# A hybrid decoder trunk on one core: the five steps of an S5 head reordered, its weight loads on another queue

## The chip, the cores and the metric

The kernel runs on one core of one Trainium2 chip. The metric is the device time of the whole kernel in microseconds (us), taken as the median of several runs; less is better. TensorE (PE; PEld is its weight load), VectorE (DVE), ScalarE (ACT) and GpSimd (POOL) each work through a list of instructions of their own; SyncE (SP) issues most of the DMA transfers.

## What is computed

One layer on a sequence of 1024 tokens of width 1024. The part that the change touches is the S5 branch, a linear recurrence with complex diagonal states; beside it stand large matrix products.

```
h = RMSNorm(x);  s5_x, s5_gate, lru_x, lru_gate, gate_s, gate_l = split(h @ W_in)
# S5: 32 groups of 16 channels, 64 complex states each
a_bar = exp(lam * dt);  b_bar = (a_bar - 1) / lam * b
state[t] = a_bar * state[t-1] + b_bar @ u[t]
y = Re(C state) + D * u
z_s = (glu(gelu(y) @ W_glu) * silu(s5_gate)) @ W_bs
z_l = (rg_lru(conv(lru_x)) * silu(lru_gate)) @ W_bl
mix = (sigmoid(gate_s) * z_s + sigmoid(gate_l) * z_l) @ W_out
x = x + RMSNorm(mix);  x = x + (p @ W_ple) * sigmoid(x @ W_ple_gate)
```

All inputs and the output are float32.

## The kernel before

**The products.** Each matrix product is built of 128x128 weight blocks. A float32 operand is split into a high part (a copy rounded to TensorE's fp32r format) and a low part (the rest), and a product is three matmuls: high by high, high by low, low by high (`three`, L327-331). The class `Weights` (from L145) loads raw weight blocks (`wraw`, L172, on SP's queue), makes the high half on ScalarE (L232) and the low half on DVE (L245) or, for some blocks, on ScalarE and a GpSimd DMA (L236, L237). Weights are made in quads of four blocks in a ring of six, four quads ahead of their use; a raw buffer comes free when the low half is made.

**The rows and the background.** `rows` computes one row of 128 output channels by 1024 tokens: eight weight blocks, two halves of 512 tokens, three matmuls each. After every second block it calls `tick()`, which advances each generator in the list `bg` by one step. All instructions of TensorE, DVE, ScalarE and GpSimd run in the order in which this code issues them, so a step of a generator lands between two pieces of a row. The order of SP's transfers is set by a planner, which places them by its own costs and due times; each waits on SP until what it needs is there. While 13 gate rows are computed (u3, two with SiLU, eight and two with a sigmoid, each followed by `light`'s sigmoid L1034 and a store L1038), the generator `s5_all` (L1008) carries the S5 branch.

**The S5 branch** in its order:
- `s5_params` (prep): small operations on the parameters. Its powers times zoh (`powers_zoh`, seven DVE operations, L681-687) go to `pzt` in page 3; GpSimd makes the input matrix `bb_1` of kernel taps with scratch `bt` (L693-695).
- `s5_ladders`: tables of cosines and sines in page 6, built by doubling (DVE, L720-729), in three pieces.
- `turn` (L699): TensorE transposes the powers (`pwT`), ScalarE copies them, and SP writes them to DRAM (`pt_d`, L706).
- `s5_load(hb)` (L892): the weights `wn` of head hb: two loads of powers from `pt_d`, replicated over 16 channels (L897), one load of B from the input `sbt` (L899), and the head's input `U` (L903). All on SP's queue; `wn` takes pages 2 and 3 in turn.
- `s5_table(hb)` (L875): cosines and sines of the head, DVE, in three steps (L883, L886-887).
- `s5_out_weights(hb)` (L909): output weights `ca`, three GpSimd products of 1.2 to 1.5 us, with scratch `t9` that shares a buffer (tag `kt`) with the tile `kt`.
- `s5_main(hb)` (L921), five steps, one a tick: (1) the product of `wn` with B (DVE, L928, L930), `dd` (GpSimd); (2) the end of the head before (`before()`: `py`, L999-1000, GELU L1002, stores of y), loads of the next head, `pkt` (L944), `pin` (L948), kernel taps `kt` copied by ScalarE (L950) and sent out in eight transfers to the Toeplitz tile `toep` (L953), a step of the next table; (3) `pq` (ScalarE, L962), rotation into `q` (DVE, L966-969), the next `ca`; (4) four scans (L976), a table step, rotation back (L980-981); (5) `q` shifted (L987-988), a table step.

There are eight heads of four groups each.

**Behind the heads** come products for six gate columns by Winograd's scheme (Strassen's with fewer additions): `lprod` on X (`xs`, copied to `lu` by ScalarE, L1145), then on Z and W. Its operands are differences T1 to T4 of quarters of h. The quarters are read back from DRAM (`h_load`, L1088); the differences are taken by `t_subs` on DVE (L1067), the high parts by `t_high` (ScalarE, L1063), the low parts by `t_low` (DVE, L1058). `t_early` does T1 and T2 from head six on, then T3 and T4; `t_build` makes the rest beside the first products. `lu` lies in page 15, which is opened over the memory that the S5 branch and the gate rows' output tiles used.

Of the kernel before, what the change touches and what calls it, by code (L numbers as in the profile page):

```python
# [17 lines left out]
P = 128  # L18
# [245 lines left out]
def tile_hybrid_trunk(  # L264
# [286 lines left out]
    def s5_params():  # L551
# [116 lines left out]
        def wide(t, sign):  # L668
            if sign:
                s_ = take(32)  # L670
                G.tensor_tensor(s_, t, sgn.to_broadcast([P, 32]), ALU.mult)
                t = s_
            return t.unsqueeze(2).to_broadcast([P, 32, 16])

# [3 lines left out]
        z_r, z_i = (t.unsqueeze(1).to_broadcast([P, 8, 32]) for t in (zr, zi))  # L678
        rv, iv = (t[:, 7::-1, :] for t in (pw_r, pw_i))
        def powers_zoh():  # L680
            V.tensor_tensor(pz[:, 0], rv, z_r, ALU.mult)  # L681
            V.tensor_tensor(pt_[:, 0], iv, z_i, ALU.mult)
            V.tensor_tensor(pz[:, 0], pz[:, 0], pt_[:, 0], ALU.subtract)
# [3 lines left out]
            V.tensor_tensor(pz[:, 1], pz[:, 1], sgn.unsqueeze(2).to_broadcast([P, 8, 32]), ALU.mult)  # L687

        turned.extend((powers_zoh, pzt))
        yield  # L690
        b1, b2, bt = (g32(braw[:, 512 * j:512 * j + 512]) for j in range(3))
        zrb, zis = wide(zr, False), wide(zi, True)
        G.tensor_tensor(bb_1, b1, zrb, ALU.mult)  # L693
        G.tensor_tensor(bt, b2, zis, ALU.mult)
# [4 lines left out]
    def turn():  # L699
        pzt = turned[1]  # L700
        ps = px.tile([P, HT], F32, tag="px", name="pwT")
        for n in range(4):
            T.transpose(ps[:, n * P:(n + 1) * P], pzt[:, n * P:(n + 1) * P], ident)
        pzs = pzt[:, 1024:1536]
        S.activation(pzs, ps, AF.Copy)
        nc.sync.dma_start(pt_d.rearrange("r (h q) (g n) -> (q g) (r h) n", h=2, n=P),  # L706
                          pzs.rearrange("p (m n) -> p m n", n=P))
# [5 lines left out]
    def s5_ladders():  # L713
        t = page(6, "etab", F32)
        e1 = t[:, :512].rearrange("p (r i n) -> p r i n", r=2, i=16)
        e2 = t[:, 512:768].rearrange("p (r i n) -> p r i n", r=2, i=16)
        tm = t[:, 768:1024].rearrange("p (r i n) -> p r i n", r=2, i=16)
        e_tab[1], e_tab[2] = e1, e2
        for e, m0, steps in ((e1, 1, 4), (e2, 5, 3)):
            V.memset(e[:, 0, :, 0:1], 1.0)  # L720
            V.memset(e[:, 1, :, 0:1], 0.0)
# [170 lines left out]
    def s5_load(hb):  # L892
        if hb > 7:
            return
        t = page(2 + hb % 2, f"wn{hb}", F32).rearrange("p (s r n) -> p s r n", s=2, r=2)
        for r in range(2):
            nc.sync.dma_start(t[:, 0, r],  # L897
                              pt_d[r, :, HT * hb:HT * hb + HT].unsqueeze(0).to_broadcast([16, 8, HT]))
# [5 lines left out]
        wload[hb] = t, U  # L904
# [16 lines left out]
    def s5_main(hb, table, before):  # L921
# [5 lines left out]
        wn, U = wload.pop(hb)  # L927
        V.tensor_tensor(wn[:, 0], wn[:, 0], wn[:, 1], ALU.mult)  # L928
        win = wn[:, 0, 0].rearrange("p (g n) -> p g n", g=4)
        V.tensor_tensor(wn[:, 0, 0], wn[:, 0, 0], wn[:, 0, 1], ALU.subtract)  # L930
        dd = wk.tile([16, 4, 16], F32, tag="dd", name=f"dd{hb}")
        G.tensor_tensor(
            dd, ident[:16, :16].unsqueeze(1).to_broadcast([16, 4, 16]),
            d_skip[:, 4 * hb:4 * hb + 4].unsqueeze(2).to_broadcast([16, 4, 16]), ALU.mult)
# [3 lines left out]
        s5_load(hb + 1)  # L938
        if hb == 7:
            h_load(2, "T2", "B22")  # L940
        kt = wk.tile([P, 576], F32, tag="kt", name=f"kt{hb}")[:16, :HT].rearrange("p (g m) -> p g m", g=4)
# [9 lines left out]
        V.tensor_tensor(kt[:, :, 0:16], kt[:, :, 0:16], dd, ALU.add)  # L951
        for j in range(8):
            nc.sync.dma_start(toep[j::8, :, 16 * j:P], kt[:, :, 0:P - 16 * j])  # L953
        if hb == 7:
            h_load(6, "T4", "B21")
        next(table, None)
        yield

        pq = wk.tile([P, 4, P], F32, tag="pq", name=f"pq{hb}").rearrange("p (r i) n -> p r i n", r=2)
# [10 lines left out]
        if hb < 7:  # L970
            s5_out_weights(hb + 1)
        yield

        for r in range(2):
# [14 lines left out]
        next(table, None)  # L989
        yield  # L990

        def finish():
            for _ in table:
                pass
# [56 lines left out]
    lop = {"T2": [3, 19], "T1": [9, 16], "T3": [17, 2], "T4": [7, 8]}  # L1051
# [13 lines left out]
    def t_subs(n, a, b):  # L1065
        for k in range(4):
            V.tensor_tensor(lf[n][:, k], lf[a][:, k], lf[b][:, k], ALU.subtract)  # L1067
            if k % 2:
                yield

    def t_early():
        yield from t_subs("T1", "T1", "T3")
        while "T2" not in lf:
            yield
        yield
        yield
        yield from t_subs("T2", "T2", "T1")
        t_high("T2")
        t_high("T1")
        lpage("T2", 1)  # L1080
        t_low("T2")
        yield
        while "T4" not in lf:
            yield
        yield from t_subs("T3", "T2", "T3")
        yield from t_subs("T4", "T4", "T2")
# [21 lines left out]
    def t_build():  # L1108
        lpage("T1", 1)
        t_low("T1")  # L1110
        yield
        t_high("T3")
        lpage("T3", 1)
        lpage("T4", 0)
        for k in range(4):
            S.activation(lop["T4"][0][:, k, :], lf["T4"][:, k], AF.Copy)
        yield
        t_low("T3")
        yield
        lpage("T4", 1)  # L1120
# [711 lines left out]
```

## Time and profile before

| | us |
|---|---|
| median of 3 runs | 941.76 (939.78 to 941.83) |
| the profiled execution, whole | 942.38 |
| its span, first to last instruction | 940.6 |
| TensorE busy | 915.2 |
| DVE busy | 664.9 |
| ScalarE busy | 493.1 |
| GpSimd busy | 150.3 |

The page of the profile gives busy times, groups of instructions by line, and the chain of work that ended last. The view of waits lists who waited for whom: engine, the waiting line, the releaser, then total us, times, and the longest. The view by stretches gives busy time per engine between two moments. A timeline row is start us, duration us, engine, line, operation, output and inputs, count, and in brackets the idle time before it and what ended it.

### The profile page before, as it was taken

The page shows a single profiled execution, that of the slowest core. Times are in us where ns is not written, and L with a number is a line of the kernel's source. Part 1 is how long each engine was busy: PE and PEld are TensorE (multiplying, and loading weights), DVE is VectorE, ACT ScalarE, POOL GpSimd, SP SyncE. Part 2 cuts the span into 40 slices and gives each one's busy share as a digit, 9 for nine tenths or more (in the row PEclk, how much of TensorE's full clock was granted, in tenths as well). Part 3 has the DMA queues.
Part 4 walks back from the last instruction along what each step waited for, and adds up shares of the span by engine and source line. Part 5 has one row for each costly group of instructions (what it writes and reads, how often), then busy time and mean ns, then how long its engine had stood idle before and what let it go on. Part 6 is the DMA issues. An engine that isn't in the chain of part 4 may idle for free.

```text
span 940.6 us, 11829 instructions
## 1 busy us (share of the span) xinstructions
PE 915.2 (97%) x4192; PEld 757.1 (80%) x4192; DVE 664.9 (71%) x1050; ACT 493.1 (52%) x763; POOL 150.3 (16%) x148
## 2 busy tenths in 40 slices
PE   9999799999989999999999999999999999999998
PEld 7887587877868888888888888888888887878887
DVE  6878787978674326777666676777863698786863
ACT  6643235434754236666666667544534255557541
POOL 1316122232100000000000000011331216522100
PEclk9999899999999999999999999999999999999999
DMA  9786656575655311111111115731469976399951
GB/s 356 299 254 209 185 158 175 142 206 171 166 154 172 101 51 49 35 46 51 51 50 51 51 45 179 253 127 34 146 213 271 257 187 206 113 241 236 273 200 64
DMA packets 76298, 146.53 MB, mean 156 GB/s; under 512 B 18896, under 2 KB 33360, under 8 KB 76240
## 3 DMA queue, kind: packets, MB, share of 16 engines
q1 hardware_dynamic: 69328, 132.68, 44.3%
q0 software_dynamic: 6768, 12.85, 7.7%
q8 instruction: 33, 0.54, 0.2%
q10 hardware_dynamic: 144, 0.26, 0.1%
q14 instruction: 25, 0.20, 0.1%
HBM read 101.06 MB, written 31.72 MB: 141 GB/s over the span
## 4 chain that ended last, share of the span: by engine, by line
PE 74%; DVE 8%; DMA 7%; issue 5%; ACT 4%; POOL 1%; SPq 0%; ACTq 0%; POOLq 0%; DVEq 0%
PE ps_rg L331 8%; PE ps_rx L331 8%; PE ps_pg L331 6%; PE ps_L L331 5%; PE ps_rx L329 4%; PE ps_rg L329 4%; PE ps_pg L329 3%; PE bZ L331 3%; PE ps_L L329 3%; PE ps_u L331 2%; DMA wn<-pt_d 2%; PE bX L331 2%; PE pg L331 2%; PE bW L331 2%; PE lZ L331 2%
## 5 line engine op out<-in xcount | busy, mean ns | idle before, releaser
L331 PE MATMUL ps_L<-hB,wq 128*128 128x512 f32 x448 | 139.3, 392 | 0.0
L232 ACT ACTIVATE wq<-wraw 128x512 fp32r<-128x512 f32 (+1 forms) x191 | 114.5, 613 | 30.0 <-DMA wraw<-w_blocks 10.3
L245 DVE TENSOR_TENSOR wq<-wraw,wq 128x512 fp32r<-128x512 f32 (+1 forms) x146 | 101.3, 709 | 14.7 <-ACT wq L232 14.7
L331 PEld LDWEIGHTS ps_L<-hB,wq 128*128 128x128 f32 x448 | 85.1, 190 | 17.9 <-DVE wq L245 0.3
L331 PE MATMUL ps_rx<-hB,wq 128*128 128x512 f32 x320 | 98.6, 389 | 0.0
L331 PE MATMUL ps_rg<-hB,wq 128*128 128x512 f32 x320 | 98.6, 389 | 0.0
L329 PE MATMUL ps_L<-hB,wq 128*128 128x512 f32 x224 | 89.0, 398 | 0.0
L331 PE MATMUL ps_pg<-x1hl,wq 128*128 128x512 f32 x240 | 74.8, 392 | 1.1 <-DMA wq<-wraw 1.1
L1212 DVE SCALAR_TENSOR_TENSOR c<-ps_rx,cp_t,c 128x1023 f32<-128x1023 f32 (+2 forms) x30 | 38.5, 1282 | 48.9 <-ACT c L1210 48.2
L331 PEld LDWEIGHTS ps_rx<-hB,wq 128*128 128x128 f32 x320 | 60.1, 188 | 12.5
L331 PEld LDWEIGHTS ps_rg<-hB,wq 128*128 128x128 f32 x320 | 60.1, 188 | 12.5
L237 POOL DMA_DIRECT2D wq<-wraw x45 | 39.6, 879 | 167.0 <-ACT wq L236 136.3
L204 POOL TENSOR_TENSOR wS<-wraw 128x512 f32<-128x512 f32 x8 | 12.2, 1519 | 333.9 <-DMA wraw<-w_blocks 322.3
L329 PE MATMUL ps_rx<-hB,wq 128*128 128x512 f32 x160 | 62.2, 389 | 0.0
L329 PE MATMUL ps_rg<-hB,wq 128*128 128x512 f32 x160 | 62.2, 389 | 0.0
L331 PEld LDWEIGHTS ps_pg<-x1hl,wq 128*128 128x128 f32 x240 | 44.9, 188 | 11.8 <-DMA wq<-wraw 2.1
L329 PEld LDWEIGHTS ps_L<-hB,wq 128*128 128x128 f32 x224 | 42.7, 190 | 8.5
L329 PE MATMUL ps_pg<-x1hl,wq 128*128 128x512 f32 x120 | 46.9, 391 | 0.0
L331 PE MATMUL ps_u<-hB,wq 128*128 128x512 f32 x128 | 39.8, 392 | 0.4 <-DVE hB L774 0.4
L331 PE MATMUL ps_F<-ys,wq 128*128 128x512 f32 x128 | 39.4, 389 | 0.0
L1220 ACT ACT_TABLE_LOAD x9 | 11.5, 1283 | 51.4 <-DVE yr L1249 51.4
L329 PEld LDWEIGHTS ps_rg<-hB,wq 128*128 128x128 f32 x160 | 30.0, 188 | 6.2
(394 smaller groups left out, 2114.5 us busy)
## 6 DMA issues: line engine op xcount, KB each, us to landing
wraw<-w_blocks SPq DMA_DIRECT2D x98, 512.0 KB
wq<-wraw POOLq DMA_DIRECT2D x45, 256.0 KB, 5.7
xt<-x_t SPq DMA_DIRECT2D x8, 512.0 KB
ple_d<-ple_sb SPq DMA_DIRECT2D x8, 512.0 KB
h_d<-xt SPq DMA_DIRECT2D x8, 512.0 KB
wn<-sbt SPq DMA_DIRECT2D x8, 512.0 KB
fT<-h_d SPq DMA_DIRECT2D x4, 1024.0 KB
wn<-pt_d SPq DMA_DIRECT2D x16, 256.0 KB
```

The costliest lines, as they stand in the source:

```text
L204: (self.nc.vector if light else G).tensor_tensor(s[name], s[a], s[b], op)
L232: nc.scalar.activation(hi, src, AF.Copy)
L237: nc.gpsimd.dma_start(lo.bitcast(F32), src, accum_op=ALU.add)
L245: self.nc.vector.tensor_tensor(lo, src, hi.bitcast(F32), ALU.subtract)
L329: T.matmul(ps, wh, xh, start=start, stop=False, skip_group_check=more)
L331: T.matmul(ps, a, b, start=False, stop=stop and a is (wh if xl_last else wl), skip_group_check=more)
L1212: V.scalar_tensor_tensor(c[:, d:], ps[:, :NT - d], w_[3 - d], c[:, d:], ALU.mult, ALU.add)
L1220: S.activation(sq, ps, AF.Sigmoid)
```

## The change

- The powers lose their seventh operation (the sign goes into two small GpSimd products ahead of them) and run inside `prep`; `bt` moves from the page of B to the second half of `pzt`, where the powers' scratch was.
- `turn` writes `pt_d` from ScalarE's queue. The loads of `wn` are split into `s5_raw` (B) and `s5_pow` (powers), both on ScalarE's queue; `U` stays on SP's.
- The ladders are dealt out in five pieces, not three.
- `t9` gets room of its own in page 6; `kt` is a plain tile.
- The five steps of a head: (1) loads of the next `wn`, a table step; (2) end of the head before, `pkt`, `pin`, `kt`, Toeplitz transfers, the next `U`, the next `ca`, a table step; (3) `pq`, `q`, the rest of the table; (4) scans, rotation back, the next `dd`; (5) `q` shifted, then the product of the next `wn`.
- One tick more ahead of the first head.
- T1 and T3 are loaded at heads one and two, T1's differences are taken one at a time at heads three to six, T2 and T4 are loaded in head six, `t_early` starts at head seven and does T2 alone; T3's and T4's differences and T1's high parts go to `t_build`.
- `lu` lies in page 9; T1's operands in pages 16 and 17, T3's in 15 and 2.

```diff
+        zrs, zis_ = take(32), take(32)
+        G.tensor_tensor(zrs, zr, sgn.to_broadcast([P, 32]), ALU.mult)
+        G.tensor_tensor(zis_, zi, sgn.to_broadcast([P, 32]), ALU.mult)
...
-            V.tensor_tensor(pz[:, 1], rv, z_i, ALU.mult)
-            V.tensor_tensor(pt_[:, 1], iv, z_r, ALU.mult)
+            V.tensor_tensor(pz[:, 1], rv, z_is, ALU.mult)
+            V.tensor_tensor(pt_[:, 1], iv, z_rs, ALU.mult)
             V.tensor_tensor(pz[:, 1], pz[:, 1], pt_[:, 1], ALU.add)
-            V.tensor_tensor(pz[:, 1], pz[:, 1], sgn.unsqueeze(2).to_broadcast([P, 8, 32]), ALU.mult)
...
+        bt = g32(pzt[:, 512:1024])
...
-        nc.sync.dma_start(pt_d.rearrange("r (h q) (g n) -> (q g) (r h) n", h=2, n=P),
+        nc.scalar.dma_start(pt_d.rearrange("r (h q) (g n) -> (q g) (r h) n", h=2, n=P),
...
-        e_tab[1], e_tab[2] = e1, e2
+        e_tab[1], e_tab[2], e_tab[9] = e1, e2, t[:, 1024:1600]
...
-                if m % 2 and m0 == 1:
+                if m and m0 == 1 or m == 1:
                     yield
...
+    def s5_raw(hb):
         t = page(2 + hb % 2, f"wn{hb}", F32).rearrange("p (s r n) -> p s r n", s=2, r=2)
-        nc.sync.dma_start(
+        nc.scalar.dma_start(
             t[:, 1].rearrange("p r n -> p (r n)"),
             sbt[:, NT * hb:NT * hb + NT].unsqueeze(1).to_broadcast([16, 8, NT]))
+        wload[hb] = t
+
+    def s5_pow(hb):
+        for r in range(2):
+            nc.scalar.dma_start(wload[hb][:, 0, r],
+                                pt_d[r, :, HT * hb:HT * hb + HT].unsqueeze(0).to_broadcast([16, 8, HT]))
+
+    def s5_u(hb):
         U = wk.tile([P, 4, P], F32, tag="U", name=f"U{hb}", bufs=2)
         nc.sync.dma_start(U, u_d[hb // 2][4 * (hb % 2):4 * (hb % 2) + 4].rearrange("g c j k -> (c j) g k"))
+        s5["U", hb] = U
+
+    def s5_in_weights(hb):
+        wn = wload[hb]
+        V.tensor_tensor(wn[:, 0], wn[:, 0], wn[:, 1], ALU.mult)
+        V.tensor_tensor(wn[:, 0, 0], wn[:, 0, 0], wn[:, 0, 1], ALU.subtract)
...
     def s5_out_weights(hb):
         if hb == 0:
-            G.tensor_tensor(cc[:, 0], cc[:, 0], sgn.to_broadcast([P, 512]), ALU.mult)
+            S.activation(cc[:, 0], cc[:, 0], AF.Identity, scale=sgn)
...
-        t9 = wk.tile([P, 576], F32, tag="kt", name=f"t9_{hb}").rearrange("p (g d c) -> p g d c", g=4, d=9)
+        t9 = e_tab[9].rearrange("p (g d c) -> p g d c", g=4, d=9)
...
     (s5_main, step 1)
+        if hb < 7:
+            s5_raw(hb + 1)
+            s5_pow(hb + 1)
+        next(table, None)
         yield
     (step 2)
         before()
-        s5_load(hb + 1)
...
+        if hb < 7:
+            s5_u(hb + 1)
+            s5_out_weights(hb + 1)
         next(table, None)
         yield
     (step 3)
-        if hb < 7:
-            s5_out_weights(hb + 1)
-        yield
-
+        for _ in table:
+            pass
+        yield
     (step 4)
+        if hb < 7:
+            s5_skip(hb + 1)
         yield
     (step 5)
-        next(table, None)
+        if hb < 7:
+            s5_in_weights(hb + 1)
         yield
...
     def s5_all():
+        s5_raw(0)
+        s5_u(0)
         for at in prep:
             if at == "trig":
                 bg.append(s5_ladders())
             yield
-        turned[0]()
         for _ in range(4):
             yield
         turn()
-        yield
-        s5_load(0)
-        h_load(7, "T1", "B12")
+        s5_out_weights(0)
+        s5_skip(0)
+        yield
+        s5_pow(0)
         yield from s5_table(0)
-        h_load(8, "T3", "B11")
-        s5_out_weights(0)
+        s5_in_weights(0)
+        yield
         before = lambda: None
         for hb in range(8):
-            if hb == 6:
+            if hb in (1, 2):
+                h_load(*((7, "T1", "B12"), (8, "T3", "B11"))[hb - 1])
+            if 2 < hb < 7:
+                V.tensor_tensor(lf["T1"][:, hb - 3], lf["T1"][:, hb - 3], lf["T3"][:, hb - 3], ALU.subtract)
+            if hb == 7:
                 bg.append(t_early())
...
-    lop = {"T2": [3, 19], "T1": [9, 16], "T3": [17, 2], "T4": [7, 8]}
+    lop = {"T2": [3, 19], "T1": [16, 17], "T3": [15, 2], "T4": [7, 8]}
...
     def t_build():
+        t_subs("T3", "T2", "T3")
+        yield
+        t_subs("T4", "T4", "T2")
+        yield
+        t_high("T1")
         lpage("T1", 1)
+        yield
         t_low("T1")
-        yield
         t_high("T3")
...
-    lu = quarter(page(15, "lu", F32))
+    lu = quarter(page(9, "lu", F32))
...
     for p_ in range(3):
-        if p_ != 1:
+        if p_ == 0:
             tick()
```

The notes in round brackets name the step that the lines belong to.

More of the change, by code (lines that the diff above doesn't have):

```diff
@@ L683, in powers_zoh @@
             V.tensor_tensor(pz[:, 0], pz[:, 0], pt_[:, 0], ALU.subtract)
-            V.tensor_tensor(pz[:, 1], rv, z_i, ALU.mult)
-            V.tensor_tensor(pt_[:, 1], iv, z_r, ALU.mult)
+            V.tensor_tensor(pz[:, 1], rv, z_is, ALU.mult)
+            V.tensor_tensor(pt_[:, 1], iv, z_rs, ALU.mult)
             V.tensor_tensor(pz[:, 1], pz[:, 1], pt_[:, 1], ALU.add)
-            V.tensor_tensor(pz[:, 1], pz[:, 1], sgn.unsqueeze(2).to_broadcast([P, 8, 32]), ALU.mult)
-        turned.extend((powers_zoh, pzt))
+        powers_zoh()
+        turned.append(pzt)
         yield
-        b1, b2, bt = (g32(braw[:, 512 * j:512 * j + 512]) for j in range(3))
-        zrb, zis = wide(zr, False), wide(zi, True)
+        b1, b2 = (g32(braw[:, 512 * j:512 * j + 512]) for j in range(2))
+        bt = g32(pzt[:, 512:1024])
+        zrb, zis = (t.unsqueeze(2).to_broadcast([P, 32, 16]) for t in (zr, zis_))
+        G.tensor_tensor(bt, b2, zis, ALU.mult)
         G.tensor_tensor(bb_1, b1, zrb, ALU.mult)
-        G.tensor_tensor(bt, b2, zis, ALU.mult)
         G.tensor_tensor(bb_1, bb_1, bt, ALU.subtract)
@@ L699, in turn @@
     def turn():
-        pzt = turned[1]
+        pzt = turned[0]
         ps = px.tile([P, HT], F32, tag="px", name="pwT")
@@ L890, in tile_hybrid_trunk, with s5_skip @@
     wload = {}
-    def s5_load(hb):
-        if hb > 7:
-            return
+    def s5_raw(hb):
         t = page(2 + hb % 2, f"wn{hb}", F32).rearrange("p (s r n) -> p s r n", s=2, r=2)
-        for r in range(2):
-            nc.sync.dma_start(t[:, 0, r],
-                              pt_d[r, :, HT * hb:HT * hb + HT].unsqueeze(0).to_broadcast([16, 8, HT]))
-        nc.sync.dma_start(
+        nc.scalar.dma_start(
             t[:, 1].rearrange("p r n -> p (r n)"),
             sbt[:, NT * hb:NT * hb + NT].unsqueeze(1).to_broadcast([16, 8, NT]))
+        wload[hb] = t
[4 more added lines that the diff above has]
+    def s5_u(hb):
         U = wk.tile([P, 4, P], F32, tag="U", name=f"U{hb}", bufs=2)
         nc.sync.dma_start(U, u_d[hb // 2][4 * (hb % 2):4 * (hb % 2) + 4].rearrange("g c j k -> (c j) g k"))
-        wload[hb] = t, U
+        s5["U", hb] = U
[3 more added lines that the diff above has]
+        V.tensor_tensor(wn[:, 0, 0], wn[:, 0, 0], wn[:, 0, 1], ALU.subtract)
+    def s5_skip(hb):
+        dd = wk.tile([16, 4, 16], F32, tag="dd", name=f"dd{hb}")
+        s5["dd", hb] = dd
+        G.tensor_tensor(
+            dd, ident[:16, :16].unsqueeze(1).to_broadcast([16, 4, 16]),
+            d_skip[:, 4 * hb:4 * hb + 4].unsqueeze(2).to_broadcast([16, 4, 16]), ALU.mult)
     def powers(t, hb, sl):
@@ L1016, in s5_all @@
         turn()
+        s5_out_weights(0)
+        s5_skip(0)
         yield
-        s5_load(0)
-        h_load(7, "T1", "B12")
+        s5_pow(0)
         yield from s5_table(0)
-        h_load(8, "T3", "B11")
-        s5_out_weights(0)
+        for _ in range(0):
+            yield
+        s5_in_weights(0)
+        yield
         before = lambda: None
         for hb in range(8):
-            if hb == 6:
+            if hb in (1, 2):
[3 more added lines that the diff above has]
+            if hb == 7:
                 bg.append(t_early())
@@ L1063, in t_high, with t_subs @@
             S.activation(lop[n][0][:, k, :], lf[n][:, k], AF.Copy)
-    def t_subs(n, a, b):
-        for k in range(4):
+    def t_subs(n, a, b, ks=range(4)):
+        for k in ks:
             V.tensor_tensor(lf[n][:, k], lf[a][:, k], lf[b][:, k], ALU.subtract)
-            if k % 2:
-                yield
     def t_early():
-        yield from t_subs("T1", "T1", "T3")
-        while "T2" not in lf:
+        yield
+        for o in (0, 2):
+            t_subs("T2", "T2", "T1", range(o, o + 2))
             yield
+        t_high("T2")
         yield
-        yield
-        yield from t_subs("T2", "T2", "T1")
-        t_high("T2")
-        t_high("T1")
         lpage("T2", 1)
         t_low("T2")
-        yield
[L1083 to L1086, printed above, removed]
     def h_load(i, t, n):
@@ L1108, in t_build @@
     def t_build():
+        t_subs("T3", "T2", "T3")
[3 more added lines that the diff above has]
+        t_high("T1")
         lpage("T1", 1)
+        yield
         t_low("T1")
-        yield
         t_high("T3")
         lpage("T3", 1)
-        lpage("T4", 0)
-        for k in range(4):
-            S.activation(lop["T4"][0][:, k, :], lf["T4"][:, k], AF.Copy)
         yield
         t_low("T3")
+        t_high("T4")
+        lpage("T4", 1)
         yield
-        lpage("T4", 1)
         t_low("T4")
```

33 lines of the change are left out of this document (9 added, 24 removed).

## The prediction

> **What bounds the kernel now.** I read the page first, then the waits of TensorE, then the busy time by stretch.
>
> ```profile
> span 940.6 us, 11829 instructions
> ```
>
> ```profile
> PE pin L948 <- issue: 6.4, 1, 6.4
> PE lX L329 <- ACT lu L1145: 4.3, 2, 2.7
> PE pin L948 <- DVE wn L930: 3.2, 4, 1.9
> PE pin L948 <- ACT ysb L1002: 1.6, 1, 1.6
> PE pwT L703 <- DVE etab L721: 1.1, 1, 1.1
> ...
> PE py L1000 <- DVE q L988: 0.7, 2, 0.5
> ```
>
> ```profile
> 60.00:104.00 44.00, 38.32 (x176) 30.81 (x174) 37.19 (x142) 15.16 (x22) 14.13 (x23) 0.98 0.67 191
> 104.00:253.00 149.00, 141.67 (x744) 118.86 (x745) 120.96 (x223) 70.19 (x125) 36.83 (x31) 0.97 0.61 174
> 253.00:275.00 22.00, 17.66 (x77) 13.99 (x76) 14.19 (x24) 14.70 (x27) 1.70 (x2) 1.00 0.56 143
> 275.00:600.00 325.00, 325.00 (x1436) 269.10 (x1435) 201.35 (x220) 199.82 (x263) 2.56 (x3) 1.00 0.27 80
> ```
>
> In a window row the pairs are busy us and count of PE, PEld, DVE, ACT and POOL; then come granted clock, DMA share and GB/s. TensorE is the bound: from 275 to 600 us it is never idle. There a matmul takes 325.00/1436 = 0.226 us, so one tick of the background work (two weight blocks, two halves, three products, 12 matmuls) is 2.72 us. No matmul is added or dropped by the change, so it can only win idle TensorE time. That is 44.00 - 38.32 = 5.7 us before 104, 7.3 us in the S5 heads and 4.3 us at the first gate products: 17.3 us, and the six rows of waits sum to the same 17.3. All six are in code that the change touches.
>
> An idle gap costs more than itself if the clock drops after it:
>
> ```profile
> 98.97 0.41 PE L944 MATMUL pkt<-ca,bb 128*16 128x128 f32 x8
> 105.82 2.05 PE L948 MATMUL pin<-U,wn 128*128 128x128 f32 x8 [6.45 <-issue]
> ...
> 109.73 0.39 PE L329 MATMUL ps_L<-hB,wq 128*128 128x512 f32 x1
> ...
> 143.30 1.13 PE L948 MATMUL pin<-U,wn 128*128 128x128 f32 x8 [1.65 <-ACT ysb L1002]
> ...
> 145.66 0.39 PE L329 MATMUL ps_L<-hB,wq 128*128 128x512 f32 x1
> ```
>
> ```profile
> 214.73 1.84 PE L948 MATMUL pin<-U,wn 128*128 128x128 f32 x8 [1.92 <-DVE wn L930]
> ...
> 218.67 0.39 PE L329 MATMUL ps_L<-hB,wq 128*128 128x512 f32 x1
> ```
>
> From pin to the third weight block behind it takes 145.66 - 143.30 = 2.36 us in the third head, but 3.91 in the first and 3.94 in the seventh. So the gap of 6.45 us costs another 1.55 and that of 1.92 another 1.58; the gap of 1.65 costs nothing more. All that can be won is 17.35 + 3.13 = 20.5 us.
>
> [...]
>
> **The change part by part.** First head (8.0 us, pin at 105.82). Its wait is put down to "issue"; DVE and SP show what was late:
>
> ```profile
> 100.07 0.42 DVE L887 TENSOR_TENSOR tt<-tt,sb 128x256 f32<-128x256 f32 x1
> 103.77 1.22 DVE L928 TENSOR_TENSOR wn<-wn 128x1024 f32<-128x1024 f32 x1 [3.28 <-DMA wn<-pt_d]
> 105.03 0.69 DVE L930 TENSOR_TENSOR wn<-wn 128x512 f32<-128x512 f32 x1
> ```
>
> ```profile
> 85.86 0.36 SPq L706 DMA_DIRECT2D pt_d<-pzt  x1
> ...
> 96.17 0.35 SPq L172 DMA_DIRECT2D wraw<-w_blocks  x1
> 96.61 1.85 SPq L897 DMA_DIRECT2D wn<-pt_d  x3
> ```
>
> ```profile
> SPq L172 <- DVE wq L245: 9.6, 2, 9.3
> ```
>
> The powers are sent to pt_d at 85.86, but the loads of wn stand on SP behind a weight load (L172) that waits 9.3 us for a raw buffer, and DVE frees that buffer late because it works through the ladders. The change puts wn's loads on ScalarE's queue, so this order is gone. What is late next is DVE: it ended the rest of the list at 100.07 + 0.42 = 100.5 without waiting. Ahead of that it now saves time, by these rows:
>
> ```profile
> 79.27 0.43 DVE L683 TENSOR_TENSOR pzt<-pzt 128x256 f32<-128x256 f32 x1
> ...
> 83.56 1.14 DVE L687 TENSOR_TENSOR pzt<-pzt,sgn 128x256 f32<-128x256 f32 x1
> ```
>
> ```profile
> 79.30 1.32 POOL L693 TENSOR_TENSOR bb<-braw,scratch 128x512 f32<-128x512 f32 x1
> ```
>
> The seventh product (L687, 1.14) is dropped; and a two-input operation on DVE takes 1.1 us and more instead of 0.43 while GpSimd runs one: L684 to L687 last from 79.27 + 0.43 to 83.56 + 1.14, 5.0 us. As bt now lies where the powers' scratch half was, GpSimd waits for the powers to be done, and three operations of 0.43 are left: 5.0 - 1.3 = 3.7 us sooner. Those GpSimd operations (three, 1.3 each) then stretch three ladder operations instead, some 0.7 each (1.14 less 0.43), so of the 3.7 I keep 1.5. The ladders in five pieces change no count. So the tables end near 99, and the product (1.22 + 0.69) near 101. One tick is put in ahead of the heads: pin comes at 98.97 + 2.72 - 1.1 (the wait of pwT, gone) + 0.3 = 100.9. What remains is 0 to 3 us; I take 0.5.
>
> Does the data get there? Two rows of what ScalarE pays and how long a load lasts:
>
> ```profile
> 0.74 0.39 ACTq L521 DMA_DIRECT2D pf<-p_t  x1
> ```
>
> ```profile
> 172.63 5.43 DMA wn<-pt_d
> ```
>
> turn() now writes pt_d from ScalarE, near 85 (85.86 less pwT's wait), and the loads follow one tick later. They must wait for that write, and the wait now stands on ScalarE itself: at most 5.4 us from 85, so to 90.4, of which the tick covers 2.7. Behind it are queued the next weight halves (made four weight quads ahead) and a gate row's sigmoid (its PSUM buffer is one of three): covered; without that cover it costs those 3 us. The loads issue by 92 and land by 97.5, ahead of DVE at 99.
>
> pwT (1.1): its third transpose waited for L687's end; the powers now end 3.7 us sooner, which is more than the wait. Gone; from 0 to 0.2 left.
>
> Heads two to eight (3.2 + 1.6 + 0.7 + 1.58 = 7.1 us). These waits end with wn's product and q, on DVE. The product stood one step ahead of pin; now it is two, 2.72 us more, against a longest wait of 1.9. And q itself was slowed:
>
> ```profile
> POOL t L918 <- DMA toep<-kt: 43.8, 4, 12.4
> ```
>
> ```profile
> 208.40 1.48 POOL L919 TENSOR_TENSOR ca<-ca,t 128x576 f32<-128x576 f32 x1
> ```
>
> ```profile
> 208.61 1.54 DVE L988 TENSOR_TENSOR q<-ta,tb 64x254 f32<-64x254 f32 x1
> ...
> 210.62 0.42 DVE L988 TENSOR_TENSOR q<-ta,tb 64x254 f32<-64x254 f32 x1
> ```
>
> ca's products on GpSimd waited up to 12.4 us for the Toeplitz copies, because their scratch shared kt's buffer; so they fell on q, just ahead of py. With a scratch of their own they run right behind py, while DVE waits for pq. There they can stretch kt's add and the table, which have a tick and more. The loads of wn are issued four ticks (10.9 us) ahead of the product; by 5.4 us for the load and three issues of 1.85/3 = 0.62, 7.3 us, they land in time. ScalarE pays 24 issues of 0.39 to 0.62, 9 to 15 us, out of 149.00 - 70.19 = 78.8 idle: covered. DVE's sum in the heads is the same but for the differences T3 and T4 (eight operations), which leave. 0 to 3 us stay; I take 0.5, since in the fourth head pin already has no wait at all:
>
> ```profile
> 160.12 1.16 PE L948 MATMUL pin<-U,wn 128*128 128x128 f32 x8
> ```
>
> First gate products (4.3):
>
> ```profile
> 261.64 0.60 ACT L1145 ACTIVATE lu<-lX 128x512 f32<-128x512 f32 x1 [5.16 <-DMA sgs_d<-sg]
> 262.14 2.18 ACT L1063 ACTIVATE lT<-fT 128x512 fp32r<-128x512 f32 x4
> ...
> 267.34 0.58 ACT L1145 ACTIVATE lu<-lX 128x512 f32<-128x512 f32 x1
> ```
>
> ScalarE could not copy the first X, since its page lay in memory that a store of the last gate row still read: 5.16 us, and then copies for T1 and T4 stood before the second X. Page 9 has no such reader, so the first two copies run at once. T1's high halves now take that wait (page 16), but behind the second X, two products on. Only the third X stands behind them, needed five products (13.6 us) after the first product begins. T3's and T4's differences (eight of DVE, 0.6 to 0.7) come into this stretch, where DVE was busy 14.19 of 22.00. Left: 0 to 4.3; I take 0.3.
>
> Sum: 20.5 - 0.5 - 0.5 - 0.3 = 19.2. The profiled execution took 942.38 for its span of 940.6; the median of the three runs is 941.76, 0.6 below. 942.4 - 19.2 = 923.2, and by the runs' median 922.6: **923.0**.
>
> **The rivals.**
> - *ScalarE's store wait returns* (T1's copies hold the third X and the weight halves behind them): up to 4.3 back, 927. For it: the same 5.16 is still there. Against: the distance of 13.6 us.
> - *SP's order still bites.* U and the Toeplitz copies stay on SP, and weight loads there still wait up to 9.3 us for buffers; T1's load comes in at head two. Half of 9.3 once: 928.
> - *DVE is the bound.* It is busy 120.96 of 149.00 in the heads; ca's products, now earlier, might push kt, pq and q as they pushed q before, and the 7.1 stays as waits elsewhere: 930. For it: the stretch of 1.1 per overlap; against: 28 us of slack.
> - *The bytes are the bound*, and the queue changes nothing: the first head's 8.0 stays, 930.5 with the 0.5 not counted twice. Against it stands the stretch in which wn was missed, where the engines were busy 0.37 of the time:
>
> ```profile
> 90.00:100.00 10.00, 9.38 (x47) 1.00 0.37 122
> ```
>
> [...]
> - *Slower: ScalarE is held by its own loads.* If each of the three issues of a head held ScalarE until landing, 3 x 5.43 = 16.3 us, that is 6.4 more than its idle 78.8/8 = 9.9 per head: 8 x 6.4 = 51 us more against 19 won, 974. It decides from 9.9 + 19.2/8 = 12.3 us of hold per head. Against: the issue at 0.74 took 0.39, not a landing's time.
> - *It does not do what it says* (the product two steps ahead still meets late data, and other waits fill in): no change, 941.
>
> **How the numbers follow.** Forecast 0.61, ScalarE's store 0.09, SP's order 0.07, DVE 0.10, bytes 0.07, no change 0.02, slower 0.04. The forecast's own range is 921.3 (all 20.5 won, by the runs' median) to 926.5. The range must take in the rivals to 930: 920.5 to 930.5, leaving out the last two and part of the 930.5 case. What a measurement can tell from no change is 0.3%, 2.8 us: faster 0.94, same 0.02, slower 0.04.
>
> **What would show it.** In TensorE's waits the rows of pin, pwT and lX should be gone or below 1 us together, and 60 to 275 us should lose some 17 us of idle time; pin's eight matmuls should take 1.13 in all heads. ScalarE should show an idle time of up to 3 us ahead of wn's first load. GpSimd's L918 should no longer wait for the Toeplitz copies. I am wrong if a pin still waits over 2 us, if py waits for the Toeplitz copies, or if lX waits for lu.

## The result and the profile after

| | before | after |
|---|---|---|
| median of the runs side by side, us | 941.8 (939.78 to 942.54, 4 runs) | 929.88 (928.2 to 933.15, 4 runs) |
| profiled execution: time, span, us | 942.38, 940.6 | 931.0, 929.2 |
| ratio of the times | | 0.9881, 95% interval 0.9848 to 0.9914 |

The change makes the kernel faster by 1.2%, some 11.4 us by the spans where 19.2 were forecast. A second set of runs of the same kernel gave 0.9845 (0.9815 to 0.9874). I read the profile after in the same order: TensorE's waits first (us in total, times, longest).

```profile
PE py L1011 <- issue: 5.0, 1, 5.0
PE pin L955 <- ACT sg L1054: 2.6, 1, 2.6
```

Of the six rows of before, four are gone without a trace: pin behind wn, pin behind ysb, pwT, and lX behind lu. Head one's wait is down from 6.4 to 2.6. But py, which had waited 0.7 in all, now waits 5.0 at one place. (Heads are counted from one here; where the list of the change gives T1's differences to heads three to six, it counts from zero, so they lie in the fourth to the seventh.) The busy time by stretch says the same:

```profile
60.00:104.00 44.00, 41.37 (x194) 33.99 (x193) 40.38 (x143) 17.46 (x25) 16.12 (x25) 1.00 0.75 219
104.00:253.00 149.00, 144.01 (x753) 120.41 (x753) 111.99 (x224) 71.31 (x126) 40.57 (x30) 0.97 0.60 174
253.00:275.00 22.00, 22.00 (x99) 18.13 (x98) 16.77 (x28) 16.60 (x32) 1.71 (x2) 1.00 0.59 162
```

TensorE's idle time from 60 to 275 us falls from 17.35 to 7.62: the gate products have none, and all of the 7.62 is the two waits. The slow clock is as large as before, at other places (granted 0.57 on the mean of the 3.89 us from pin on, and 0.50 in the 3.68 us from py to the next pkt):

```profile
103.02 1.53 PE L955 MATMUL pin<-U,wn 128*128 128x128 f32 x8 [2.63 <-ACT sg L1054]
104.21 0.77 PE L329 MATMUL ps_L<-hB,wq 128*128 128x512 f32 x1
...
106.91 0.44 PE L329 MATMUL ps_L<-hB,wq 128*128 128x512 f32 x1
...
208.83 0.76 PE L1011 MATMUL py<-U,toep 128*128 128x128 f32 x2 [4.99 <-issue]
...
212.51 0.53 PE L951 MATMUL pkt<-ca,bb 128*16 128x128 f32 x8
```

From pin to the third weight block behind it takes 106.91 - 103.02 = 3.89 us instead of 2.36. From py to the next pkt takes 212.51 - 208.83 = 3.68; one head earlier, where py did not wait, it took 1.88. That is 1.53 + 1.80 = 3.3 us.

Two questions follow. What made py wait in the sixth head and the product in the first? And which of the edits took the other waits away?

**VectorE in head one.** First its rows, then GpSimd's, in the same stretch of the changed kernel:

```profile
85.79 1.41 DVE L723 TENSOR_TENSOR etab<-etab,cosp 128x256 f32<-128x256 f32 x1
87.12 1.44 DVE L724 TENSOR_TENSOR etab<-etab,sinp 128x256 f32<-128x256 f32 x1
88.60 1.40 DVE L725 TENSOR_TENSOR etab<-etab 128x128 f32<-128x128 f32 x1
89.92 2.75 DVE L726 TENSOR_TENSOR etab<-etab 128x128 f32<-128x128 f32 x1
...
100.98 1.21 DVE L908 TENSOR_TENSOR wn<-wn 128x1024 f32<-128x1024 f32 x1
```

```profile
85.69 1.23 POOL L929 TENSOR_TENSOR ca<-pw,cc 128x576 f32<-128x576 f32 x1 [1.50 <-ACT cc L923]
...
88.36 1.49 POOL L931 TENSOR_TENSOR ca<-ca,etab 128x576 f32<-128x576 f32 x1
...
90.11 1.21 POOL L929 TENSOR_TENSOR ca<-pw,cc 128x576 f32<-128x576 f32 x1
91.29 1.22 POOL L930 TENSOR_TENSOR etab<-pw,cc 128x576 f32<-128x576 f32 x1
```

GpSimd makes ca of head one at 85.69, and from 90.11 on all of ca of head two as well, a whole head early: its scratch no longer waits for anything. (Before the change, ca of head one lay under the ladders too, at 84.50, but of head two only the first product, at 88.74.) Under the products shown, operations of VectorE last 1.4 us; the last of these four spans two products, 2.75. The product of wn starts at 100.98 and waited for no data, and VectorE's rows show no gap ahead of it from 80 us on. The view names ScalarE as pin's releaser, but pin's 103.02 lies right behind the end of wn's second operation, 102.23 + 0.69 = 102.92.

**The sixth head.** Rows of GpSimd, VectorE, SP, ScalarE's queue and TensorE:

```profile
188.81 1.68 POOL L929 TENSOR_TENSOR ca<-pw,cc 128x576 f32<-128x576 f32 x1 [11.44 <-PE py L1012]
189.33 1.44 DVE L880 TENSOR_TENSOR tt<-etab 128x256 f32<-128x256 f32 x1
190.69 1.45 DVE L880 TENSOR_TENSOR sb<-etab 128x256 f32<-128x256 f32 x1
192.06 1.92 DVE L245 TENSOR_TENSOR wq<-wraw,wq 128x512 fp32r<-128x512 f32 x1
193.90 0.21 DVE L958 TENSOR_TENSOR kt<-kt,dd 16x64 f32<-16x64 f32 x1
...
194.43 2.57 SPq L1016 DMA_DIRECT2D y_d<-ysb  x4
197.43 5.39 SPq L960 DMA_DIRECT2D toep<-kt  x8
200.63 0.55 ACTq L891 DMA_DIRECT2D wn<-sbt  x1
201.37 1.18 ACTq L898 DMA_DIRECT2D wn<-pt_d  x2
```

```profile
204.00:208.80 4.80, 0.00 (x0) 0.00 (x0) 2.35 (x5) 0.00 (x0) 0.00 (x0) 0.71 1.01 289
```

Three operations of VectorE ahead of kt's add take 1.44, 1.45 and 1.92 under GpSimd's products of the next head's ca. A weight load (L172) stands on SP until 194.0, when VectorE has freed its buffer; then come y's four stores, then the Toeplitz copies: the first is issued 197.43 - 189.07 (pin) = 8.4 us behind pin. While they are under way, 1 MB of wn's loads goes out on ScalarE's queue. The window row is the stretch in which TensorE does nothing: the DMA engines are all busy (share 1.01). Its wait is put down to "issue"; I take it that py waited for the last copy, whose issue ended 208.83 - 202.82 = 6.0 us earlier. In the runs gate1, lu15 and wn8late the same wait has the copies as its releaser (4.2, 4.6 and up to 3.7 us).

My theory after this: (1) the scratch of its own lets ca run ahead under VectorE's work, which delays the product in head one and the copies in the sixth head; (2) the late copies then meet wn's loads, which the other queue sends without regard to them. Rivals: lateness alone is enough; VectorE is late without GpSimd; the bytes bound the stage.

### The profile page after: what moved, and what is told of

It reads as the page before. It is cut to its first block, busy times and chain, and to the rows that moved or that the text cites. A ratio compares the mean times of both kernels' runs of the same rounds, so it can differ in the third digit from the quotient of the medians.

```text
span 929.2 us, 11782 instructions
## 1 busy us (share of the span) xinstructions
PE 913.4 (98%) x4192; PEld 755.5 (81%) x4192; DVE 655.2 (71%) x1049; ACT 493.5 (53%) x764; POOL 155.3 (17%) x148
## 4 chain that ended last, share of the span: by engine, by line
PE 78%; issue 8%; DMA 6%; DVE 5%; POOL 1%; ACT 1%; SPq 1%; POOLq 0%; ACTq 0%; DVEq 0%
PE ps_L L331 10%; PE ps_rx L331 8%; PE ps_rg L331 8%; PE ps_L L329 5%; PE ps_rg L329 4%; PE ps_rx L329 4%; PE ps_u L331 3%; PE ps_pg L331 2%; PE bZ L331 2%; PE bW L331 2%; PE bX L331 2%; PE pg L331 2%; DMA msr<-ms_d 2%; PE lZ L331 2%; PE ps_ea L331 2%
## 5 line engine op out<-in xcount | busy, mean ns | idle before, releaser
L331 PEld LDWEIGHTS ps_L<-hB,wq 128*128 128x128 f32 x448 | 84.7, 189 | 17.7
L331 PEld LDWEIGHTS ps_rg<-hB,wq 128*128 128x128 f32 x320 | 60.1, 188 | 12.4
```

What stands on the lines that cost most here:

```text
L331: T.matmul(ps, a, b, start=False, stop=stop and a is (wh if xl_last else wl), skip_group_check=more)
```

## The experiments

Every set of runs had the kernel before beside it (median 942.2 to 944.1 us). Ratios with their intervals stand in the table; times are medians of four runs (six for the last).

| run | edit | us | ratio (95%) | pin, head one | py, largest |
|---|---|---|---|---|---|
| again | none | 929.91 | 0.9845 (0.9815 to 0.9874) | 3.0 | 4.8 |
| gate | ca behind kt's add, all heads | 924.75 | 0.9795 (0.9771 to 0.9820) | 1.0 | 0.7 |
| yact | y's stores on ScalarE's queue | 927.63 | 0.9829 (0.9803 to 0.9856) | 2.6 | 2.8 |
| wnsp | wn's loads on SP | 924.27 | 0.9795 (0.9764 to 0.9825) | 3.4 | 0.4 |
| gate_wnsp | both | 922.80 | 0.9785 (0.9756 to 0.9813) | 0 | 0.2 |
| wn8late | the last wn load two steps later | 931.13 | 0.9872 (0.9845 to 0.9900) | 3.0 | 3.7 |
| gate1 | the gate for the second head's ca | 927.36 | 0.9821 (0.9794 to 0.9849) | 1.1 | 4.2 |
| gate6 | for the eighth head's ca | 931.39 | 0.9872 (0.9836 to 0.9907) | 2.6 | 3.9 |
| gate5 | for the seventh head's ca | 925.50 | 0.9816 (0.9785 to 0.9846) | 3.1 | 0.8 |
| gate15 | second and seventh | 922.36 | 0.9780 (0.9754 to 0.9806) | 1.6 | 0.8 |
| lu15 | copies of X on page 15 again | 932.71 | 0.9889 (0.9864 to 0.9913) | 3.1 | 4.6 |
| prod1 | product one step ahead again | 931.76 | 0.9878 (0.9850 to 0.9907) | 3.0 | 5.9 |
| prod1_wnsp | that and wn's loads on SP | 925.53 | 0.9803 (0.9775 to 0.9830) | 3.6 | none |
| t9kt | ca's scratch in kt's buffer again | 927.78 | 0.9836 (0.9802 to 0.9870) | 1.1 | 2.1 |
| bt9 | before, with only the scratch moved | 937.29 | 0.9944 (0.9924 to 0.9965) | 6.1 | none |

The eight runs of the changed kernel, in both sets, lie between 928.2 and 933.15 us. All runs of gate, wnsp, gate_wnsp, gate1, gate5, gate15 and prod1_wnsp lie below that; those of yact, wn8late, gate6, lu15, prod1 and t9kt overlap with it, so for these the waits say more than the total.

**Three ways to cure py.** The unchanged kernel was run again beside them:

> The changed kernel once more, nothing edited. In its first profile two waits are left: pin of head one (2.6 us, and a slower clock behind it) and py of head six (5.0 us, and a slower clock behind it). Theory A (order: the Toeplitz copies of head six are sent late, since on SP they stand behind y's stores and a weight load that waits for DVE, and DVE is stretched by GpSimd's ca products): the same two waits at the same places, 3 to 7 us together with clock 8 to 11, 927 to 933 us. Rival N (chance of a single execution): the py wait is gone or at another head, and the time is spread as before.

It shows the same two waits at the same places, so they belong to the kernel and not to one execution. "gate" makes dd of the next head ahead of ca's products, in the step in which these stand, and dd waits for kt's add:

```
             s5_u(hb + 1)
+            s5_skip(hb + 1)
             s5_out_weights(hb + 1)
...
-        if hb < 7:
-            s5_skip(hb + 1)
         yield
```

> GpSimd's dd of the next head moves ahead of its ca products, so ca's products wait until kt's add of this head is done (dd has one buffer). Theory A: kt's add is no longer stretched (0.2 us instead of 1.0) and comes within 2.3 us of pin's start in heads two to seven, against 2.8 and in head six 4.8; py's wait in head six falls from 5.0 to under 1.5; and as head two's ca cannot run under the ladders any more, pin of head one waits 0.5 to 1.5 instead of 2.6: 921 to 925 us. Rival B (the bytes: wn's loads on the second queue share the 16 engines with the Toeplitz copies and slow them): py's wait in head six stays over 3 us, 926 to 928. Rival D (DVE has too much to do in any order): ca's products now stretch the rotations, q comes late and py waits for q instead, 3 us and more at one or more heads, 927 to 931.

"yact" takes only y's stores out of SP's order ahead of the copies (issued behind the next head's copies of kt on ScalarE):

```
-                nc.sync.dma_start(y_d[b][:, g0 + g], ysb[:, g])
+                    nc.scalar.dma_start(y_d[b][:, g0 + g], ysb[:, g])
```

> y's four stores of a head go to ScalarE's queue, behind kt's copies, so that SP has 2.6 us less ahead of the Toeplitz copies. Theory A: the copies of head six are sent 2 to 3 us sooner, py's wait there falls from 5.0 to 0 to 2.5; 923 to 927 us, pin of head one unchanged at 2.6. Rival B: the same bytes move at the same time, py's wait stays at 4 to 5 us, 928 to 931. Rival D: unchanged too, as DVE's list is the same.

"wnsp" takes back the queue of wn's three loads a head, at the places that the change gives them:

```
-        nc.scalar.dma_start(
+        nc.sync.dma_start(
...
-            nc.scalar.dma_start(wload[hb][:, 0, r],
+            nc.sync.dma_start(wload[hb][:, 0, r],
```

> Only the loads of wn go back to SP's queue, in the places that the changed kernel gives them; pt_d's write stays on ScalarE. Theory A (the first head's wait came from SP's order): pin of head one waits 6 us and more again, as the loads stand behind a weight load that waits for DVE; 933 to 938 us. In the heads the loads then stand in one line with the Toeplitz copies and py may wait more or less by 3 us. Rival B: the queue makes no difference to the first head (2.6 us), but the copies of head six no longer share the engines with wn's loads and py's wait there goes: 921 to 925 us.

The gate takes both waits down and wins 5.2 us over the unchanged kernel; y's stores take about half of py's wait. The surprise is wnsp: with the loads back on SP the kernel is 5.6 us faster, so the move to ScalarE's queue, taken alone, costs time. Its rows in the sixth head:

```profile
197.85 5.10 SPq L960 DMA_DIRECT2D toep<-kt  x8
...
204.36 0.38 PE L1011 MATMUL py<-U,toep 128*128 128x128 f32 x2
...
206.25 0.57 SPq L891 DMA_DIRECT2D wn<-sbt  x1
```

The copies go out just as late behind pin (8.1 us), but wn's loads stand behind them on the one queue, and py finds its copies landed at most 1.4 us after the last issue. A start 8 us behind pin is not enough by itself for the long wait. In head one, where I had put the queue's gain, it is 3.4 against 2.6 to 3.0: under 1 us.

> Both edits together: the next head's ca waits for this head's Toeplitz add, and wn's loads are back on SP's queue. Theory (py's wait at head six needs both late copies and wn's loads beside them; the product's wait in head one is VectorE under GpSimd's ca of head two): each edit alone takes nearly all of py's 5 us, so the two do not add there: py waits under 0.8 us, and TensorE's wait at the product of head one is 1.0 to 2.5 us (1.0 with the gate alone, 3.4 with SP's queue alone): 921 to 925. Rival 1 (two independent costs of about 5.5 us each): 918 to 920. Rival 2 (the bytes or the issue count bound the stage): no better than either alone, 924 to 926, with a wait of over 2 us that moves to another head.

The two edits do not add (922.8 against 924.8 and 924.3, intervals that overlap): two cures of one wait, as the theory has it. Head one has no wait at all here: with VectorE not held up, it frees the raw buffer sooner, SP's weight load waits 7.1 us instead of 10.9 in wnsp, and the order on SP no longer bites. With the gate and ScalarE's queue, head one waits 1.0.

**Lateness or meeting.** Only the last wn load is moved:

```
-        if hb < 7:
+        if hb < 6:
             s5_raw(hb + 1)
             s5_pow(hb + 1)
...
         if hb == 6:
+            s5_raw(7)
+            s5_pow(7)
             h_load(2, "T2", "B22")
```

> Only the eighth head's wn load and powers move, from step 1 to step 3 of the head before; everything else as in the changed kernel. Theory (the late Toeplitz copies lose to the 1 MB of wn's loads that ScalarE's queue sends at the same time): the copies land in under 4 us behind their issue, py's wait at 209 goes from 4.9 to under 1 us, and the time to 924 to 926; the product of head one keeps its wait of 2.6 to 3.0. Rival 1 (the copies' late issue is enough by itself): py still waits over 3 us, 928 to 930. Rival 2: the last head's product now waits for its wn, TensorE loses 2 to 5 us there, and the time is 926 to 930 although py no longer waits.

```profile
199.40 6.13 SPq L960 DMA_DIRECT2D toep<-kt  x8
...
206.90 0.46 PE L1013 MATMUL py<-U,toep 128*128 128x128 f32 x2 [1.13 <-DMA toep<-kt]
...
221.00 5.10 SPq L960 DMA_DIRECT2D toep<-kt  x8
...
227.71 0.46 PE L1013 MATMUL py<-U,toep 128*128 128x128 f32 x2 [3.72 <-DMA toep<-kt]
```

In the sixth head the copies are as late as before (8.4 us behind pin), and land 1.4 us after the last issue instead of 6.0: the wait falls from 5.0 to 1.1. So meeting the loads makes up most of it; lateness by itself leaves the 1.1. The time did not fall, which I had not expected: the seventh head's copies now go out 11.8 us behind pin, SP having waited 7.1 us for another load, and py waits 3.7 there although they land 1.6 us behind the last issue. So lateness alone can do it too, if it is large enough. The wait moved, and the total says nothing against the theory.

**Single gates.** The same gate for one head's ca each (gate1: the second head's; gate6: the eighth's; gate5: the seventh's), then both that worked:

> Only the second head's ca waits for the first head's Toeplitz add; the other heads stay as in the changed kernel. Theory (the three GpSimd products of head two's ca, which run ahead under the first head's ladders, stretch VectorE by some 2 to 3 us): TensorE's wait at the first product falls from 2.6-3.0 to about 1.0 us, py's wait of 5 us stays, 927 to 929. Rival (the stretch comes from the first head's own ca and bb alone, or the data lands late): the wait stays above 2.4 us, 929.5 to 930.5.

> Only the eighth head's ca waits for the seventh head's Toeplitz add. Theory (these three GpSimd products stretch VectorE's table rows and the weight rounding ahead of the Toeplitz add, so that the copies leave some 4 us later and meet wn's loads): the copies are issued about 3 to 4 us earlier behind the product, py's wait of 4.9 us goes to under 1 us, with about 2 us of slow clock, 923 to 925; the first product's wait of 2.6 to 3.0 stays. Rival 1 (VectorE is late there by itself): the wait stays above 3 us, 929 to 931. Rival 2 (the wait moves to another head): 926 to 929.

> The gate at the place that the run before it missed by a head: only the seventh head's ca waits for the sixth head's Toeplitz add. Theory (these GpSimd products stretch VectorE ahead of that add, so the copies leave some 3 to 4 us later and meet wn's loads): py's wait goes to under 1 us, with some 2 us of slow clock behind it, and the first product's wait of 2.6 to 3.0 stays: 924 to 926. Rival 1 (VectorE is late there without GpSimd too): the wait stays above 3 us, 929 to 931. Rival 2 (the wait moves to the next head): 926 to 929.

> Both single gates, for the second and the seventh head's ca; wn's loads stay on ScalarE's queue. Theory (two separate causes of one kind, GpSimd's products under VectorE's work): the first product waits about 1.0 us, py under 1 us, and the time is that of the gate in all heads, 922.5 to 925. Rival (the gate in the other heads matters too): 925.5 to 928.

gate1, head one of VectorE:

```profile
90.23 0.51 DVE L724 TENSOR_TENSOR etab<-etab,sinp 128x256 f32<-128x256 f32 x1
...
90.98 0.29 DVE L726 TENSOR_TENSOR etab<-etab 128x128 f32<-128x128 f32 x1
...
99.72 1.22 DVE L908 TENSOR_TENSOR wn<-wn 128x1024 f32<-128x1024 f32 x1 [0.99 <-DMA wn<-pt_d]
```

Without ca of head two, the last two ladder operations shown take 0.29; VectorE is done with the tables at 98.7 and waits for wn's data. The pin wait is 1.1. gate6 put the gate one head late, and the sixth head's copies still leave 8.4 us behind pin. gate5 stands at the right place:

```profile
189.69 0.42 DVE L880 TENSOR_TENSOR tt<-etab 128x256 f32<-128x256 f32 x1
190.03 0.41 DVE L880 TENSOR_TENSOR sb<-etab 128x256 f32<-128x256 f32 x1
190.36 0.68 DVE L245 TENSOR_TENSOR wq<-wraw,wq 128x512 fp32r<-128x512 f32 x1
...
194.50 6.65 SPq L960 DMA_DIRECT2D toep<-kt  x8
...
204.90 0.46 PE L1013 MATMUL py<-U,toep 128*128 128x128 f32 x2 [0.70 <-issue]
```

The same three operations take 1.5 us instead of 4.8, the copies go out 5.1 us behind pin instead of 8.4, and py waits 0.7 although wn's loads are still beside them (they land 3.75 us behind the last issue). gate15 has both effects, 922.36 us: 7.5 less than the changed kernel in the runs, and the 923.0 of the forecast. The gate in the other heads wins nothing; in "gate" pin waits 1.2 us behind wn in three heads, a wait that gate15 does not have.

**Which edit won the rest.** Undone one at a time:

```
-    lop = {"T2": [3, 19], "T1": [16, 17], "T3": [15, 2], "T4": [7, 8]}
+    lop = {"T2": [3, 19], "T1": [16, 17], "T3": [9, 2], "T4": [7, 8]}
...
-    lu = quarter(page(9, "lu", F32))
+    lu = quarter(page(15, "lu", F32))
```

> Only the copies of X go back to page 15 and T3's high halves to page 9. My prediction: the wait of 4.3 us of the first gate products behind lu returns, 933 to 935. Rival (the later heads free page 15 early enough now that TensorE reaches the gate products later against GpSimd): under 1 us returns, 929.5 to 931.

```profile
PE lZ L329 <- ACT lu L1174: 1.1, 1, 1.1
...
PE lX L329 <- ACT lu L1159: 0.4, 1, 0.4
```

1.5 us of waits return, not 4.3 (the median is 2.8 higher, with runs that overlap); the rest of that wait does not come back with page 15. What else took it I did not try. "prod1" calls the product (s5_in_weights) at the start of the step of its own head again, "prod1_wnsp" does that with wnsp:

```
-        if hb < 7:
-            s5_in_weights(hb + 1)
         yield
...
+        if hb:
+            s5_in_weights(hb)
```

> Only the wn product goes back one step (one tick ahead of its head instead of two). My prediction: pin's waits for wn in the heads two to eight return, 3 us in all, and with them some slow clock: 932 to 935. Rival 1 (ScalarE's and VectorE's rows lie differently now, so the product ends in time one step later as well): 929 to 931. Rival 2 (VectorE is freed in the steps in which the Toeplitz copies were late, so py's wait shrinks): below 929.

> The product one step ahead again and wn's loads on SP's queue, both as before the change; ladders, ca's products, pages as in the changed kernel. Theory A (my prediction's: product and queue are what took the 7.1 us out of heads two to eight, and each covers for the other): the waits of pin behind wn return, 2 to 4 us in all, 926 to 929. Theory B (what took them out is that ca's GpSimd products left q's place, so q and the product end in time one step ahead too): under 1 us returns, 924 to 925.5.

One pin waits 0.6 us behind wn in the first, 0.5 in the second. The two edits that I had credited with heads two to eight can both be taken back for half a microsecond of waits (by the medians, 925.5 against wnsp's 924.3, with runs that overlap). So the scratch was tried from both sides: put back in the changed kernel, and moved alone in the kernel before.

```
-        t9 = e_tab[9].rearrange("p (g d c) -> p g d c", g=4, d=9)
+        t9 = wk.tile([P, 576], F32, tag="kt", name=f"t9_{hb}").rearrange("p (g d c) -> p g d c", g=4, d=9)
```

> Only the scratch of ca's products shares the Toeplitz buffer again, as before the change. Theory (the scratch of its own is what lets ca run early, under the ladders in head one and under the table in head seven): both waits shrink, the first product's to 1.0-1.5 and py's at 209 to under 1 us; but ca falls on q again as before, which puts 1 to 3 us of waits at py or pin into other heads: 924 to 928. Rival (ca's place is not the cause of either wait): both stay, and q's waits come on top, 930 to 933.

```
-        e_tab[1], e_tab[2] = e1, e2
+        e_tab[1], e_tab[2], e_tab[9] = e1, e2, t[:, 1024:1600]
...
-        t9 = wk.tile([P, 576], F32, tag="kt", name=f"t9_{hb}").rearrange("p (g d c) -> p g d c", g=4, d=9)
+        t9 = e_tab[9].rearrange("p (g d c) -> p g d c", g=4, d=9)
```

> The kernel before the change with one edit: the scratch of ca's products in the table's page, as the change puts it, instead of in the Toeplitz buffer. Theory B (what freed the heads two to eight is that ca left q's place): of pin's waits behind wn and ysb and py's behind q, 5.5 us in all, under 2 us are left, with the first head's 6.4 and the gate products' 4.3 as they were: 935 to 938. Theory A (product two steps ahead and the other queue did it): over 4 us are left, 940 to 943. Theory C: as in the changed kernel, ca's products run ahead and a wait of 2 to 5 us appears at a py: 938 to 942, with pin's waits gone.

With the scratch back, ca falls on q again (py behind q 1.3, pkt behind ca 1.6) and head one's wait is 1.1: both sides of the edit in one profile. In the changed kernel the two about cancel: 927.78 against 929.91, with runs that overlap. Moved alone in the kernel before, the scratch leaves of pin's and py's 5.5 us this:

```profile
PE pin L948 <- issue: 6.1, 1, 6.1
...
PE pin L948 <- DVE wn L930: 1.3, 2, 0.9
```

4.2 us of these waits are gone by that one edit. The first head's row is nearly as it was, with a new wait of 2.3 beside it (a weight half that VectorE makes), where ca now runs under the ladders. Net, TensorE's idle time from 60 to 275 us falls from 17.35 to 14.35, the span by 3.4, and the medians differ by 5.0 (0.9944). The sixth head's copies leave 4.5 us behind pin in this run (4.4 in the kernel before), and py does not wait. So the scratch alone does not make them late; it takes the new order of the five steps as well, and which part of that order, no run shows. Nor was any run made that takes back the powers, the ladders in five pieces or the extra tick, so what brought head one's wait from 6.4 to 2.6 is not shown edit by edit; the queue's part is under 1 us.

## Why the forecast fell short

**The ceiling and the bound held.** TensorE's waits are what the change moved, and every row that I named as "gone" went, or shrank. gate15 shows that the forecast's level can be had by this change plus two gates. Of the three signs of being wrong that I had named, two came: a pin waits over 2 us (2.6), and py waits for the Toeplitz copies (5.0).

**"First head (8.0)" failed by a size.** I had 0.5 us left; it is 2.6. The step was "of the 3.7 I keep 1.5", by three stretched ladder operations. The powers did end early (80.4 instead of 84.7), but from there to the end of the tables VectorE took 101.05 - 80.43 = 20.6 us instead of 100.49 - 84.70 = 15.8: 4.8 more, where the step allowed 2.2, and the tables ended at 101.05 instead of "near 99". bb's three operations were counted; the two products of ca of head two that now run under the ladders as well were not. Without ca of head two there (gate1), VectorE ends the tables at 98.7, and 1.1 us are left. The other half of the step, that ScalarE's queue is what frees wn's loads, fell: on SP the wait is 3.4 instead of about 3, and with the gate it is 0 on SP and 1.0 on ScalarE's queue. SP's wait there was for a buffer that VectorE frees, so it shrank with VectorE's lateness (10.9 us in wnsp, 7.1 in gate_wnsp). In the load's way, pt_d took 91.47 - 84.77 = 6.7 us from the end of its issue to the next load, where I had at most 5.4, and ScalarE had nothing to do from 86.1 to 91.5, 5.3 us where I had "up to 3". Both hid behind VectorE; with the gate, where VectorE is done early, it waits 1.67 us for wn's data (0.99 in gate1), and that is the 1.0 to 1.1 left at pin.

```profile
84.37 0.40 ACTq L703 DMA_DIRECT2D pt_d<-pzt  x1
...
91.47 1.18 ACTq L898 DMA_DIRECT2D wn<-pt_d  x2
```

**"Heads two to eight (7.1)" had the right sum for the wrong edit, and missed a price.** The rows went, but mainly through the scratch (4.2 of 5.5 us by that edit alone), not "product two steps ahead". The sentence that failed is "there they can stretch kt's add and the table, which have a tick and more". They have not, in the sixth head: SP's order behind kt's add has a weight load and four stores ahead of the copies, T1's difference stands on VectorE there too, and beside wn's loads the copies land later behind their last issue (6.0 us by py's start, against at most 1.4 in wnsp). I had worked out whether wn's loads land in time (they do), and not what they do to the copies on the other queue. That was the largest error: 5.0 us of wait and 1.8 of slow clock, where the sum had 0.5. Of my rivals, "the bytes are the bound" and "DVE is the bound" each held half of it, at one place instead of throughout. That the 929.9 lies so near their 930 and 930.5 is luck: neither the first head's 8.0 nor the 7.1 of the heads stayed, and new waits of like size came in.

The runs show the price of the second queue: 5.6 us lost by the move alone (929.88 against wnsp's 924.27), since the one queue had kept the small urgent copies ahead of the 1 MB. VectorE's stretch has its price in the rows: 0.42 becomes 1.41 to 1.45 beside GpSimd products of 1.2 to 1.7 us. What makes VectorE slower there was not shown.

**"First gate products (4.3)" held in the outcome**: ScalarE copies the first two X at once.

```profile
251.66 0.59 ACT L1159 ACTIVATE lu<-lX 128x512 f32<-128x512 f32 x1
...
253.18 0.59 ACT L1159 ACTIVATE lu<-lX 128x512 f32<-128x512 f32 x1
```

But taking page 9 back returns only 1.5 of it, so that much is shown to be its work. **pwT** went as worked out.

**The slow clock** I had let go with the waits; 3.3 us of it came back with the two new ones.

**The sum.** Waits 7.6 instead of 1.3 and slow clock 3.3 instead of 0 make 9.6 us short of 19.2; the spans differ by 11.4, so the loss is 7.8. The 1.8 between them lie in no row that I found, and are within the spread of the runs of one kernel (928.2 to 933.15).

## What to carry to other kernels

When an edit takes away a wait on one engine, list what that engine will now do earlier and which engine's operations it will run beside: a buffer that held GpSimd back was also what kept it off VectorE's critical list. Before you give large loads a queue of their own, look for small transfers with a deadline that the shared queue had kept ahead of them. And undo the edits one at a time: here the two with the longest argument could be taken back for 0.5 us of waits together, while a line about a scratch buffer took 4.2 us of waits out of the old kernel and brought two new ones into the new.

## What the runs showed of the hardware

In these runs a gap's length alone did not tell whether the clock drops behind it. The gaps ahead of pin in head one were 3.04 us in the second run of the changed kernel, with slow matmuls behind it, and 3.05 in gate5, with none:

```profile
103.76 1.13 PE L955 MATMUL pin<-U,wn 128*128 128x128 f32 x8 [3.04 <-ACT sg L1054]
```

```profile
104.11 1.13 PE L955 MATMUL pin<-U,wn 128*128 128x128 f32 x8 [3.05 <-ACT sg L1056]
```

The granted clock says the same (the third number from the end; the first pair is TensorE's busy time). First a stretch behind pin in the second run of the changed kernel, then one that holds pin in gate5:

```profile
104.89:108.30 3.41, 3.41 (x9) 2.65 (x9) 3.41 (x8) 2.14 (x5) 0.74 (x1) 0.50 0.54 150
```

```profile
102.85:106.26 3.41, 2.15 (x14) 1.95 (x15) 3.38 (x9) 1.91 (x5) 0.74 (x1) 1.00 0.72 258
```

It was 0.50 in the one and 1.00 in the other. In the kernel before, the mean granted clock from pin to the third weight block behind it was 0.57 behind the gaps of 6.45 and 1.92 us (105.82 to 109.73 and 214.73 to 218.67), and 1.00 behind that of 1.65 (143.30 to 145.66). From 60 to 900 us the clock was at half at two places in each of the two profiles: from 102.32 to 109.15 and from 214.96 to 218.37 before, from 103.59 to 107.00 and from 205.99 to 212.82 after the change. What decides it beside the gap's length was not shown. So what a gap costs behind itself is read here from the granted clock and the matmuls behind it.
